# The compression network's second product behind three steps of s4, modulation out of s5, and more zero products at the seams

## The chip, the cores and the metric

The kernel runs on one core of a Trainium2 chip. The metric is device time in microseconds of one execution: the median of three runs before the change is 848.4 us (848.1, 848.4 and 856.6). Times below are us from the start of the span of one profiled execution unless said otherwise.

## The reference

Two layers work on x of 256 rows x 1024 columns in f32. One layer, cut to what matters here:

```python
h = rmsnorm(x) * (1 + scale) + shift          # scale, shift, gates: modulation, c @ adaw + adab
z = h @ w_in                                  # one input projection, its columns feed three mixers
ret  = retention(z)                           # 4 heads x 64
gmlp = spatial_gating(z)                      # 4 groups x 64, chunks of 128
nsa  = sparse_attention(z)                    # 8 query heads, 2 key heads: compressed, selected, window
x = x + gate * (concat(ret, gmlp, nsa) @ w_out)
h = rmsnorm(x) * (1 + scale2) + shift2
x = x + gate2 * experts(h)                    # 16 experts, best group of 4, top 2 in it, each 512 wide
```

The compressed branch of sparse attention runs a small network over blocks of keys and values (first product, gelu, second product) and scores the queries against its output.

## The kernel before, in words

All weights come from HBM in f32, through one queue (SP) that issues its transfers in a fixed order into a ring of eleven slots of 1 MB (`slot`, L100 to L104); a transfer waits until the readers of the slot that it overwrites are done. Further transfers of the same queue fill the experts' `wd` tiles (L1267, L1270).

A product with a weight is made of three (`mm3`, L349 to L352), since the weight and the activation are each split into a rounded part and a rest. `whl` (L338 to L347) makes the split: ACT casts the upper part (L344), DVE, or POOL for every third piece, takes the rest (L346); five such pieces can be live. The input projection is cut into pieces s0 to s5. s0 to s4 have the weight as the stationary operand and eight steps of twelve products each (`dz`); s5 has the activation stationary and 280 columns.

The order around the change, in each layer: the sum of squares (`rms_r`, L311 to L323: ACT's squares L316, PE's sums `pm` L317, ACT's logarithm L321 and exponential L322, then `hhi` L421), s0 to s3, the compression network (`comp`: first product `ph` L539, second `ph2` L544, gelu on DVE with `hid` as its result L137, third `pk` L551 with its rotary norm L357 and L360 and the values' product `pv` L564), s5, then attention. `scores(j)` (L640 to L656) makes the window scores of head pair j, `cmp_soft` (`pcs` L603) the compressed ones, `retention` its own (`pin` L695, `por` L705), `cmp_turn` transposes the compressed weights (`pct` L625), `values(j)` transposes the weights (L664, L670) and applies them (L680, L684). A string per layer, `S4P`, gives the number of s4's steps behind each half of these four rounds. Then come the output projection (`pw`), the router, the ranking of the tokens (`prank` L936 to L940), the gather (`pgx` L980), the experts (`pgu` L1051, `py` L1084) and the combination (L1123, L1131, L1310).

The modulation (c @ adaw) is cut into tasks; most are two DVE products of 128x1024 each (L193) and an addition (L194), some are PE products (L209). `FILL`, a table of digits per layer and stage, says where a task is handed out. A scheduler then orders each engine's instructions by their dependences and priorities, so the tables set priorities and not the places themselves. `WARM` times four is the number of zero products (L948) ahead of the ranking. At the seam between the layers a list `fence` names the last instructions of layer 0 on POOL, ACT and DVE; ACT's and DVE's splits of layer 1 are issued behind them.

Of the kernel before, what the change touches and what calls it, by code (L numbers as in the profile page):

```python
# [17 lines left out]
S = 256  # L18
# [22 lines left out]
OFL = True  # L41
WARM = (1, 6)
WV = (0, 1, 5)
NPA = ("0011", "0011")
S4P = ("01111111", "01111111")
WP = (3, 3)
# [16 lines left out]
         "s0 s1 s2 cmp s3 a11.0 a11.1 s5 a11.2 a11.3 s4 a12.0 a12.1 o1 o0 a12.2 a12.3".split()]  # L63
FILL = [["00000000", "00000000", "10101010", "10100000", "00", "21212121", "2222000000000000", 0],
        ["01010101", "01010101", "00000000", "00101010", "00", "10101010", "2222000000000000", 0, "000000000000000000000000"]]

# [9 lines left out]
def trunk(tc, I, out):  # L76
    nc = tc.nc
    P = 128
# [4 lines left out]
    with ctx:  # L83
# [224 lines left out]
        def tables(after):  # L308
            with tc.issue_after(after):
                exp_ln_tables()  # L310

        def rms_r(l, src, last=None):
            pm = bank("W", "pm")
            for c in range(8):
                sq = tl("k1", [S], "sq")
                sq_ = A.activation(sq, src[:, c, :], AF.Square)  # L316
                T.matmul(pm[:, :S], onesd, sq, start=c == 0, stop=c == 7)  # L317
            if last is not None:
                last(sq_.ins)
            r = tl("k1", [S], "r")  # L320
            A.activation(r, pm[:, :S], AF.Ln, bias=epsc[:, 0:1])  # L321
            A.activation(r, r, AF.Exp, scale=-0.5)  # L322
            return r  # L323
# [14 lines left out]
        def whl(wv, n):  # L338
            hl = tl("wh", [2, 512], "whl", F32R)
            hi, lo = hl[:, 0, :n], hl[:, 1, :n]  # L340
            with contextlib.ExitStack() as st:
                for i_ in fence[1:]:
                    st.enter_context(tc.issue_after(i_))
                A.copy(hi, wv)  # L344
                wc[0] += 1
                (G if wc[0] % WP[fl[0]] == 0 else V).tensor_tensor(lo, wv, hi.bitcast(F32), op=OP.subtract)  # L346
            return hi, lo  # L347

        def mm3(o, a, b, start, stop):  # L349
            T.matmul(o, a[0], b[0], start=start, stop=False, skip_group_check=True)  # L350
            T.matmul(o, a[0], b[1], start=False, stop=False, skip_group_check=True)  # L351
            T.matmul(o, a[1], b[0], start=False, stop=stop, skip_group_check=True)  # L352

# [20 lines left out]
        for l in range(L):  # L374
# [30 lines left out]
            if True:  # L405
# [33 lines left out]
                def small_loads(after):  # L439
                    with tc.issue_after(after):  # L440
                        A.dma_start(wsT, I["ws"][l].rearrange("p (g t) -> p g t", g=4))
                        A.dma_start(bsv, I["bs"][l].rearrange("p (t n) -> p t n", t=2))
                        if l == 0:
# [5 lines left out]
                                    fill=0.0, base=0, pattern=[[0, 4], [1, P]], channel_multiplier=-1)  # L449

                def dz(idx, dst_fn, tag="D"):
                    pz = [bank(tag, "pz") for _ in range(2)]

                    def step(c):
                        w = whl(ld[f"s{idx}"][c // 4][:, 512 * (c % 4):512 * (c % 4) + 512], 512)
                        for t in range(4):
                            d = slice(P * t, P * t + P)
                            mm3(pz[t // 2][:, S * (t % 2):S * (t % 2) + S], (w[0][:, d], w[1][:, d]),
                                (hhi[:, c, :], hlo[:, c, :]), c == 0 and t % 2 == 0, c == 7)
                        if c == 7:  # L460
                            for t in range(2):
                                dst_fn(2 * t, pz[t].rearrange("p (u n) -> p u n", u=2))
                    return step
# [69 lines left out]
                def comp():  # L533
# [7 lines left out]
                    raw = tl("k1", [P], "raw")  # L541
                    A.copy(raw, ph[:, :P])
                    ph2 = bank("W", "ph2")
                    T.matmul(ph2[:, :64], raw, csel.rearrange("p v g n -> p (v g n)"), start=True, stop=True)  # L544
                    hid = sml([64], "hid")
                    gelu(hid, ph2[:, :64], [64])
                    hidv = hid.rearrange("p (v g n) -> p v g n", v=2, g=2)
                    w2 = smv(l, "w2").rearrange("p (v d) -> p v d", v=2)
# [10 lines left out]
                    for g in range(2):  # L559
# [7 lines left out]
                                    hm.rearrange("p j h -> p (j h)").unsqueeze(2).to_broadcast([P, 8, 64]), op=OP.mult)  # L567
                    return bd

# [18 lines left out]

                bd = comp()
                gv = tl("t2", [2, 256], "gv")  # L590
                gat = sml([2, 24], "gat")

                def s5(tt, pz):
                    sigm(gat[:, tt, :], pz[:, 256:280])
                    gelu(gv[:, tt, :], pz[:, :256], [256])
                run(tm(5, 280, s5), lambda c: fill(FILL[l][1][c]))
                gatv = gat.rearrange("p t (h b) -> p t h b", b=3)
# [131 lines left out]
                def s4_step(n=1):  # L729
                    for _ in range(int(n)):  # L730
# [4 lines left out]
                        s4c[0] += 1  # L735

                pj = {0: scores(0)}
                cs = cmp_soft()
                for j in range(4):
# [101 lines left out]
def moe(tc, nc, l, env):  # L841
# [19 lines left out]
    if True:  # L861
# [264 lines left out]
        def combine_few(yy, pT):  # L1126
            for u in range(2):
                for i in range(2):
                    for q in range(4):
                        r_ = slice(SW * q, SW * q + SW)  # L1130
                        T.matmul(mo[q][:, S * u:S * u + S], yy[i][r_, P * u:P * u + P], pT[r_, :], start=False, stop=False,  # L1131
                                 skip_group_check=True)

# [174 lines left out]
        for m in (0, 2, 4, 6, 1, 3, 5, 7):  # L1308
            b, u = m // 2, m % 2
            last[1] = V.scalar_tensor_tensor(xT[:, m, :], mo[b][:, S * u:S * u + S], mod(l, 5)[:, m:m + 1], xT[:, m, :],  # L1310
                                   op0=OP.mult, op1=OP.add).ins
        return [last[2]] + last[:2]

# [75 lines left out]
```

## Time and profile before

| | us |
|---|---|
| median of three runs | 848.4 |
| the profiled execution | 856.05 |
| its span, first to last instruction | 854.5 |
| PE busy | 762.8 (89%) |
| DVE busy | 459.3 (54%) |
| ACT busy | 273.4 (32%) |
| POOL busy | 68.0 (8%) |
| mean granted clock of PE | 0.929 |

The profiled execution's own time stands 1.55 us above its span. PE's clock has two levels, 2.4 GHz (1.00) and 1.2 GHz (0.50); a value between is a mean over a stretch with both. "Busy" PE is PE with a product under way, at either clock. An idle time in brackets names the instruction whose end came last; a product of f32 operands appears as two records (x4 for two products).

### The profile page before, as it was taken

To read this page: it belongs to the slowest core of one execution; us is meant where nothing else is said; L and a number is where in the kernel's file an instruction comes from. 1 tells how busy PE (TensorE), PEld (TensorE's weight loads), DVE (VectorE), ACT (ScalarE), POOL (GpSimd) and SP (SyncE) were. 2 spreads that over 40 slices of the span, in tenths; PEclk is the share of its full clock that TensorE was granted. 3 is DMA by queue.
4 is the path that set the end of the run, shared out by engine and by line. 5 is a ranking of instruction groups with operands and counts; after the bars stand their busy time and mean duration, and the time that the engine had idled before them with its cause. 6 is when DMAs were issued, how large, how long until landed. Compare 5 with 4: busy or idle time off the path is not lost. (4 is left out here: it accounts for less than half of the span.)

```text
span 854.5 us, 14344 instructions
## 1 busy us (share of the span) xinstructions
PE 762.8 (89%) x5460; PEld 480.2 (56%) x5460; DVE 459.3 (54%) x1189; ACT 273.4 (32%) x655; POOL 68.0 (8%) x83
## 2 busy tenths in 40 slices
PE   3789999976999999887988998999999999979795
PEld 2677665775535455343448886678744545534342
DVE  6997959986833223211245998598582322312123
ACT  6246555633111111110135646466311201101010
POOL 2232200120000000000003231002000000000000
PEclk9899869979899999989999996699999999998798
DMA  8959818979799999999999489178878999999993
GB/s 354 420 224 354 321 45 296 395 275 383 304 381 418 417 418 419 418 420 413 421 417 379 156 300 389 58 265 323 318 283 303 359 421 415 419 418 418 416 418 145
DMA packets 47169, 292.95 MB, mean 343 GB/s; under 512 B 5488, under 2 KB 6256, under 8 KB 16496
## 3 DMA queue, kind: packets, MB, share of 16 engines
q1 hardware_dynamic: 45648, 289.76, 85.3%
q10 hardware_dynamic: 1440, 2.16, 0.8%
q8 instruction: 46, 0.75, 0.3%
q14 instruction: 35, 0.29, 0.1%
HBM read 290.84 MB, written 1.05 MB: 342 GB/s over the span
## 5 line engine op out<-in xcount | busy, mean ns | idle before, releaser
L1051 PE MATMUL pgu<-w1slot,xg 128*64 128x512 f32 x640 | 168.5, 623 | 18.3 <-PEq L1188 9.8
L1051 PEld LDWEIGHTS pgu<-w1slot,xg 128*64 128x64 f32 x640 | 51.7, 141 | 101.0 <-issue 97.9
L193 DVE SCALAR_TENSOR_TENSOR adaslot<-adaslot,sb__90 128x1024 f32<-128x1024 f32 x72 | 94.5, 1324 | 0.0
L1093 DVE SCALAR_TENSOR_TENSOR yy<-py,gc,yy 64x512 fp32r<-64x512 f32 x40 | 30.0, 750 | 108.6 <-ACT yy L1092 108.6
L350 PE MATMUL pz<-hhi,whl 128*128 128x256 f32 x256 | 75.0, 304 | 10.2 <-ACT hhi L421 10.2
L351 PE MATMUL pz<-hlo,whl 128*128 128x256 f32 x256 | 76.1, 301 | 0.9 <-DVE hlo L422 0.7
L352 PE MATMUL pz<-hhi,whl 128*128 128x256 f32 x256 | 76.3, 304 | 0.5 <-DVE whl L346 0.4
L1092 ACT ACTIVATE yy<-py,gc 64x512 fp32r<-64x512 f32 x40 | 27.3, 683 | 151.5 <-PE py L1084 135.3
L346 POOL TENSOR_TENSOR whl<-winslot,whl 128x512 fp32r<-128x512 f32 (+1 forms) x24 | 34.2, 1425 | 370.7 <-DMA winslot<-win_dram 239.7
L1060 PE MATMUL pgu<-w1slot,xg 128*32 128x256 f32 x896 | 58.4, 382 | 5.2 <-DMA w1slot<-w_dram 5.2
L350 PEld LDWEIGHTS pz<-hhi,whl 128*128 128x128 f32 x256 | 51.1, 205 | 14.4 <-ACT hhi L421 13.1
L351 PEld LDWEIGHTS pz<-hlo,whl 128*128 128x128 f32 x256 | 52.5, 205 | 3.0 <-DVE hlo L422 1.7
L352 PEld LDWEIGHTS pz<-hhi,whl 128*128 128x128 f32 x256 | 51.9, 204 | 3.6 <-issue 2.1
L1040 DVE CAST pgT<-ppg 128x256 fp32r<-128x256 f32 x34 | 14.4, 424 | 72.3 <-PE ppg L1038 72.3
L344 ACT CAST whl<-winslot 128x512 fp32r<-128x512 f32 (+1 forms) x72 | 40.7, 576 | 26.6 <-PE pz L352 25.4
L1067 DVE TENSOR_TENSOR a<-a,pgu 128x256 f32<-128x256 f32 (+1 forms) x34 | 12.4, 365 | 65.6 <-ACT a L1066 65.4
L1060 PEld LDWEIGHTS pgu<-w1slot,xg 128*32 128x32 f32 x896 | 28.6, 109 | 33.8 <-issue 16.5
L1066 ACT ACTIVATE a<-pgu 128x256 f32<-128x256 f32 (+1 forms) x34 | 11.6, 340 | 108.4 <-PE pgu L1051 91.7
L350 PE MATMUL pw<-yhi,whl 128*128 128x256 f32 x128 | 37.6, 295 | 5.5 <-DVE mod L194 3.9
L1101 ACT ACTIVATE yy<-py,gc 128x256 fp32r<-128x256 f32 x14 | 6.6, 473 | 108.6 <-PE py L1109 108.6
L346 DVE TENSOR_TENSOR whl<-winslot,whl 128x512 fp32r<-128x512 f32 (+1 forms) x48 | 33.7, 707 | 10.0 <-ACT whl L344 9.9
L352 PE MATMUL pw<-yhi,whl 128*128 128x256 f32 x128 | 36.9, 295 | 2.3 <-DVE whl L346 2.2
(506 smaller groups left out, 1455.7 us busy)
## 6 DMA issues: line engine op xcount, KB each, us to landing
w1slot<-w_dram SPq DMA_DIRECT2D x128, 1024.0 KB, 16.2
adaslot<-adaw_dram SPq DMA_DIRECT2D x40, 1024.0 KB, 7.0
wd<-wd_dram SPq DMA_DIRECT2D x30, 1024.0 KB, 14.7
winslot<-win_dram SPq DMA_DIRECT2D x14, 1024.0 KB, 16.1
slot<-adaw_dram SPq DMA_DIRECT2D x8, 1024.0 KB, 18.5
woslot<-wout_dram SPq DMA_DIRECT2D x8, 1024.0 KB, 11.6
slot<-win_dram SPq DMA_DIRECT2D x6, 1024.0 KB, 17.5
cmpslot<-cmpw_dram SPq DMA_DIRECT2D x4, 1024.0 KB, 13.5
```

The lines of the kernel that those rows point to most:

```text
L193: V.scalar_tensor_tensor(wb, wb, 1.0, sb_, op0=OP.mult, op1=OP.mult, accum_out=mv_[:, b:b + 1])
L344: A.copy(hi, wv)
L346: (G if wc[0] % WP[fl[0]] == 0 else V).tensor_tensor(lo, wv, hi.bitcast(F32), op=OP.subtract)
L350: T.matmul(o, a[0], b[0], start=start, stop=False, skip_group_check=True)
L351: T.matmul(o, a[0], b[1], start=False, stop=False, skip_group_check=True)
L352: T.matmul(o, a[1], b[0], start=False, stop=stop, skip_group_check=True)
L1040: V.tensor_copy(pT, pp_[:, :S])
L1051: lastu[0] = T.matmul(gu[64 * j:64 * j + 64, :], xg(c)[:, xs:xs + CAP], w1(c, j), start=c == 0, stop=c == 7, skip_group_check=True).ins
L1060: lastu[0] = T.matmul(gu[SW * t:SW * t + SW, 0:256], xg(c)[:, xs:xs + SW], wv, start=c == 0, stop=c == 7, skip_group_check=True).ins
L1067: V.tensor_tensor(a, a, gu[:, n:2 * n], op=OP.mult)
L1092: ya = A.activation(y[0:64, :], py[r_, :], AF.Copy, scale=gc[r_, :])
L1093: V.scalar_tensor_tensor(y[64:128, :], py[r_, :], gc[r_, :], y[0:64, :].bitcast(F32), op0=OP.mult, op1=OP.subtract)
```

## The change

The second half of the compression network moves. `comp` becomes a generator of three parts: the first product before s5; the second product and the gelu after the first step of s5; `pk` and what follows behind three steps of s4 that now stand before scores(0), with a fence on the last product of the third. A fourth step of s4 follows scores(0), and three more are left for the rounds. `FILL` takes the modulation out of s5 in layer 1 and hands tasks out between s4's steps. `WARM` makes 24 zero products of 4 in layer 0, and 32 of 24 in layer 1. A new helper `spin` puts three zero products ahead of the seam's sums of squares and eight behind them. The fence of the splits on ACT is now the last of the eight squares.

```diff
-WARM = (1, 6)
+WARM = (6, 8)
-S4P = ("01111111", "01111111")
+S4P = ("11010000", "11010000")
-FILL = [["00000000", "00000000", "10101010", "10100000", "00", "21212121", "2222000000000000", 0],
-        ["01010101", "01010101", "00000000", "00101010", "00", "10101010", "2222000000000000", 0, "000000000000000000000000"]]
+FILL = [["00000000", "00000000", "00001111", "10100000", "00", "21212121", "2222000000000000", 0],
+        ["01010101", "00000000", "00010111", "00101010", "00", "10101010", "2222000000000000", 0, "000000000000000000000000"]]
...
+        def spin(n, after):
+            wz = bank("W", "wz")
+            with tc.issue_after(after):
+                for _ in range(n):
+                    T.matmul(wz, zb, zb.unsqueeze(1).to_broadcast([P, 4, P]), start=True, stop=True, skip_group_check=True)
+
         def rms_r(l, src, last=None):
+            if fence:
+                spin(3, fence[3])
             pm = bank("W", "pm")
             for c in range(8):
                 sq = tl("k1", [S], "sq")
                 sq_ = A.activation(sq, src[:, c, :], AF.Square)
-                T.matmul(pm[:, :S], onesd, sq, start=c == 0, stop=c == 7)
+                pm_ = T.matmul(pm[:, :S], onesd, sq, start=c == 0, stop=c == 7)
             if last is not None:
                 last(sq_.ins)
+            if fence:
+                fence[1] = sq_.ins
+                spin(8, pm_.ins)
...
-                for i_ in fence[1:]:
+                for i_ in fence[1:3]:
...
                     raw = tl("k1", [P], "raw")
                     A.copy(raw, ph[:, :P])
+                    yield
                     ph2 = bank("W", "ph2")
                     T.matmul(ph2[:, :64], raw, csel.rearrange("p v g n -> p (v g n)"), start=True, stop=True)
                     hid = sml([64], "hid")
                     gelu(hid, ph2[:, :64], [64])
+                    yield
                     hidv = hid.rearrange("p (v g n) -> p v g n", v=2, g=2)
...
-                bd = comp()
+                bds = []
+                cgen = comp()
+                next(cgen)
...
-                run(tm(5, 280, s5), lambda c: fill(FILL[l][1][c]))
+
+                def comp_step(c):
+                    if c == 0:
+                        next(cgen)
+                run(tm(5, 280, s5), lambda c: fill(FILL[l][1][c]), comp_step)
...
+                s4_step(3)
+                with tc.issue_after(ls4[0]):
+                    next(cgen, None)
+                bd = bds[0]
                 pj = {0: scores(0)}
+                s4_step(1)
                 cs = cmp_soft()
...
-        return [last[2]] + last[:2]
+        return [last[2]] + last[:2] + [lastu[0]]
```

`lastu[0]` is the last product of the combination; `ls4[0]` is the last product that `mm3` returned in a step. Line numbers below 300 are the same in both kernels; further down those of the changed one are 8 to 26 higher.

PE's order in layer 0 between s5 (`pz<-whl,hlo`) and the first scores (`sc<-kr,qn`); before:

```order
L352 MATMUL pz<-whl,hlo 128x280
L695 MATMUL pin_1242<-rr 128x256
L551 MATMUL pk<-hid,sm_67 64x15 x2
L695 MATMUL pin_1243<-rr 128x256
L357 MATMUL pr<-zc,pg 128x15
L360 MATMUL pm_1020<-sqc,bo 128x15
L695 MATMUL pin_1242<-rr 128x128
L695 MATMUL pin_1243<-rr 128x128
L564 MATMUL pv<-sm_67,hvr 128x64
L640 MATMUL sc_1142<-kr,qn 128x256
```

and after, where `pz<-hhi,whl` and `pz<-hlo,whl` are s4's products (twelve such groups of three stand ahead of `pk`, three behind it):

```order
L363 MATMUL pz<-whl,hlo 128x280
L361 MATMUL pz<-hhi,whl 128x256
L362 MATMUL pz<-hlo,whl 128x256
L363 MATMUL pz<-hhi,whl 128x256
...
L566 MATMUL pk<-hid,sm_67 64x15 x2
...
L368 MATMUL pr<-zc,pg 128x15
L371 MATMUL pm_1167<-sqc,bo 128x15
L579 MATMUL pv<-sm_67,hvr 128x64
L661 MATMUL sc_1189<-kr,qn 128x256
```

36 products of s4 have moved ahead of `pk`, and retention's products (`pin`) behind the scores. Up to the first `pct` there are 72 products of s4 (31 before) in layer 0 and 81 (28 before) in layer 1.

SP's order in layer 0 ahead of the experts' first weights (`w1slot`), where `adaslot` is the modulation's, `woslot` the output projection's; before:

```order
L103 DMA winslot<-win_dram 128x2048 x2
L103 DMA adaslot<-adaw_dram 128x2048 x9
L1267 DMA wd__2185<-wd_dram 128x1024
L103 DMA adaslot<-adaw_dram 128x2048
L103 DMA woslot<-wout_dram 128x2048 x4
L103 DMA adaslot<-adaw_dram 128x2048 x12
L103 DMA w1slot<-w_dram 128x2048 x4
L1267 DMA wd__2187<-wd_dram 128x1024
```

and after, where the same tile is `wd__2205` by its new number:

```order
L103 DMA winslot<-win_dram 128x2048 x2
L103 DMA adaslot<-adaw_dram 128x2048 x10
L103 DMA woslot<-wout_dram 128x2048 x4
L103 DMA adaslot<-adaw_dram 128x2048 x12
L103 DMA w1slot<-w_dram 128x2048 x4
L1293 DMA wd__2205<-wd_dram 128x1024
L1293 DMA wd__2207<-wd_dram 128x1024
```

The issue of that tile has moved behind 17 slots of the modulation and the output projection and four of the experts.

ACT's order at the seam between the layers, where `sq<-xT` are the squares, `whl<-winslot` the splits' casts, `r` the logarithm and the exponential; before:

```order
L344 CAST whl<-winslot 128x512 x2
L316 ACTIVATE sq<-xT 128x256
L344 CAST whl<-winslot 128x512 x2
L316 ACTIVATE sq<-xT 128x256 x7
L140 ACT_TABLE_LOAD
L344 CAST whl<-winslot 128x512
L321 ACTIVATE r<-pm,epsc 128x256
L322 ACTIVATE r<-r 128x256
L421 ACTIVATE hhi<-ht,mod_118 128x256 x6
```

and after:

```order
L324 ACTIVATE sq<-xT 128x256 x8
L140 ACT_TABLE_LOAD
L355 CAST whl<-winslot 128x512
L332 ACTIVATE r<-pm,epsc 128x256
L355 CAST whl<-winslot 128x512
L333 ACTIVATE r<-r 128x256
L355 CAST whl<-winslot 128x512 x2
L432 ACTIVATE hhi<-ht,mod_118 128x256 x4
```

The eight squares stand together; the four casts that stood among them are behind.

## Rows read from the trace of the kernel before

**Rows 1.** Busy time by stage: us, engines busy (instructions), PE's clock, DMA share, GB/s.
```profile
98.00:128.00 30.00, 28.64 (x109) 17.45 (x109) 20.00 (x62) 16.10 (x63) 1.60 (x2) 0.66 0.37 155
128.00:168.00 40.00, 39.17 (x307) 27.87 (x305) 37.53 (x96) 24.89 (x76) 2.89 (x3) 1.00 0.90 341
...
222.00:441.00 219.00, 201.28 (x1553) 98.28 (x1549) 64.76 (x204) 30.08 (x58) 0.00 (x0) 0.98 1.00 407
...
518.00:552.00 34.00, 31.18 (x115) 21.23 (x115) 21.79 (x67) 19.49 (x70) 4.46 (x3) 0.60 0.46 182
```
**Rows 2.** PE's timeline, layer 0: start, length, operation, [idle before <-releaser].
```profile
97.94 0.29 PE L352 MATMUL pz<-whl,hlo 128*128 128x280 f32 x1
...
100.21 0.29 PE L551 MATMUL pk<-hid,sm 128*64 128x15 f32 x4 [1.35 <-DVE hid L137]
...
103.37 1.23 PE L640 MATMUL sc<-kr,qn 64*128 64x256 f32 x4
...
109.59 3.46 PE L603 MATMUL pcs<-kcr,qn 128*128 128x32 f32 x16
...
123.57 0.28 PE L350 MATMUL pz<-hhi,whl 128*128 128x256 f32 x1
123.68 0.28 PE L351 MATMUL pz<-hlo,whl 128*128 128x256 f32 x1
...
128.14 0.38 PE L625 MATMUL pct<-ident,cs 128*128 128x128 f32 x2
...
133.87 0.70 PE L640 MATMUL sc<-kr,qn 64*128 64x256 f32 x4
...
136.24 1.05 PE L209 MATMUL pad<-adaslot,scol 128*32 128x512 f32 x2
```
**Rows 3.** PE's timeline, layer 1, s5's last product, pk and pct.
```profile
517.41 0.29 PE L352 MATMUL pz<-whl,hlo 128*128 128x280 f32 x1
...
520.83 0.38 PE L551 MATMUL pk<-hid,sm 128*64 128x15 f32 x4 [3.12 <-DVE hid L137]
...
552.45 0.38 PE L625 MATMUL pct<-ident,cs 128*128 128x128 f32 x2
```
**Rows 4.** DVE's timeline, a split of s4 (layer 0) and the modulation ahead of hid (layer 1).
```profile
99.34 0.68 DVE L346 TENSOR_TENSOR whl<-winslot,whl 128x512 fp32r<-128x512 f32 x1
...
519.32 1.21 DVE L193 SCALAR_TENSOR_TENSOR adaslot<-adaslot,sb__90 128x1024 f32<-128x1024 f32 x1
```
**Rows 5.** Waits of SP's queue: us in total, times, longest.
```profile
SPq L103 <- DVE adaslot L193: 100.8, 24, 27.6
...
SPq L1267 <- PE pin L695: 23.1, 1, 23.1
```
**Rows 6.** PE's timeline at the entry to the experts, both layers.
```profile
209.88 0.38 PE L948 MATMUL mo<-zb 128*128 128x512 bf16 x1 [0.73 <-DVE lg L873]
213.90 0.17 PE L936 MATMUL prank<-o,ub 128*128 128x16 bf16 x1 [3.64 <-DVE o L924]
...
221.52 1.07 PE L1051 MATMUL pgu<-w1slot,xg 128*64 128x512 f32 x3
...
613.58 4.69 PE L948 MATMUL mo<-zb 128*128 128x512 bf16 x21
618.71 0.17 PE L936 MATMUL prank<-o,ub 128*128 128x16 bf16 x1 [0.44 <-DVE o L924]
...
623.98 0.65 PE L1051 MATMUL pgu<-w1slot,xg 128*64 128x512 f32 x2
```
**Rows 7.** Timelines of ACT and PE at the seam between the layers.
```profile
450.18 0.47 ACT L321 ACTIVATE r<-pm,epsc 128x256 f32<-128x256 f32 x1 [1.30 <-PE pm L317]
...
452.21 0.50 PE L350 MATMUL pz<-hhi,whl 128*128 128x256 f32 x2 [2.07 <-ACT hhi L421]
...
455.80 0.39 PE L350 MATMUL pz<-hhi,whl 128*128 128x256 f32 x1
```
**Rows 8.** Busy time in a stretch of layer 1 with PE idle for 1.45 us.
```profile
616.00:620.00 4.00, 2.55 (x17) 1.14 (x15) 3.76 (x32) 2.03 (x4) 0.00 (x0) 1.00 0.97 359
```

More of the change, by code (lines that the diff above doesn't have):

```diff
@@ L351, in mm3 @@
             T.matmul(o, a[0], b[1], start=False, stop=False, skip_group_check=True)
-            T.matmul(o, a[1], b[0], start=False, stop=stop, skip_group_check=True)
+            return T.matmul(o, a[1], b[0], start=False, stop=stop, skip_group_check=True).ins
         def rope_norm(pool, xs, sq, n, nt, gcol, pg, cos, sin, outs, sumidx, eps):
@@ L449, in small_loads @@
                                     fill=0.0, base=0, pattern=[[0, 4], [1, P]], channel_multiplier=-1)
+                ls4 = [None]
                 def dz(idx, dst_fn, tag="D"):
@@ L457, in step @@
                             d = slice(P * t, P * t + P)
-                            mm3(pz[t // 2][:, S * (t % 2):S * (t % 2) + S], (w[0][:, d], w[1][:, d]),
-                                (hhi[:, c, :], hlo[:, c, :]), c == 0 and t % 2 == 0, c == 7)
+                            ls4[0] = mm3(pz[t // 2][:, S * (t % 2):S * (t % 2) + S], (w[0][:, d], w[1][:, d]),
+                                         (hhi[:, c, :], hlo[:, c, :]), c == 0 and t % 2 == 0, c == 7)
                         if c == 7:
@@ L567, in comp @@
                                     hm.rearrange("p j h -> p (j h)").unsqueeze(2).to_broadcast([P, 8, 64]), op=OP.mult)
-                    return bd
+                    bds.append(bd)
                 if l or LK < 1:
@@ L1130, in combine_few @@
                         r_ = slice(SW * q, SW * q + SW)
-                        T.matmul(mo[q][:, S * u:S * u + S], yy[i][r_, P * u:P * u + P], pT[r_, :], start=False, stop=False,
-                                 skip_group_check=True)
+                        lastu[0] = T.matmul(mo[q][:, S * u:S * u + S], yy[i][r_, P * u:P * u + P], pT[r_, :], start=False,
+                                            stop=False, skip_group_check=True).ins
         def extras():
```

## The prediction

> **What bounds the kernel now.** I read the busy times by stage first, then PE's timeline where a stage's clock is low, then the waits of PE and SP there. In [rows 1] the expert stage of layer 0 (222 to 441 us) moves 407 GB/s with the DMA engines busy 1.00 of the time: the weight stream bounds it, and the diff changes neither it nor its like in layer 1. What can move is what lies before each stream: the stream's first product comes as soon as attention and routing let it, and the stream then runs its own length. Two stretches there stand out. From 98 to 128 us PE is "busy" 28.64 of 30 us at a granted clock of 0.66, while DVE has 20.00 us of work and the DMA engines 0.37. From 518 to 552 us it is the same in layer 1: PE 31.18 of 34 us at clock 0.60, DVE 21.79, DMA 0.46. So there PE is full only because it runs at 1.2 GHz, and no other engine is near its limit. Right behind, from 128 to 168 us, PE has 39.17 of 40 us at clock 1.00 and DVE 37.53: both nearly full, so a gain made before is carried through, and not much more is to be had.
>
> PE's timeline [rows 2] shows how the first stretch begins: the last product of s5 starts at 97.94 (0.29 us), and pk of the compression network starts at 100.21 after 1.35 us of waiting for DVE's hid (the products of retention between them are short). What follows is narrow (15 columns) and then the scores, and all of this runs at half clock: scores(0) takes 103.37 to 109.59 = 6.2 us; the same four products of scores(2) at full clock take 133.87 to 136.24 = 2.4 us. In layer 1 [rows 3] s5's products stop at 517.41 and pk waits 3.12 us for hid; the transposes of the weights (pct) that end the stretch come at 552.45. On DVE [rows 4] hid stands behind a modulation product of 1.21 us (at 519.32).
>
> **The change part by part.** The sums are against the profiled execution, 856.05 us (span 854.5 and 1.55 us around it); it lies 7.6 us (0.9%) above the median of the three runs, 848.4, and the saving is carried to the median in us.
>
> *Layer 0, opening of attention.* pk no longer stands behind s5, but behind three steps of s4, 36 products. At full clock these start 0.115 us apart (123.57 and 123.68, [rows 2]), so they fill 36 x 0.115 = 4.1 us, from 98.2 to 102.3, past the time at which hid is there today (pk starts at 100.21). Up to the first pct 72 products of s4 now stand in PE's order, 31 before: 41 x 0.115 = 4.7 us of work is brought forward. If the clock stays at 2.4 GHz, the stretch from s5's end (98.2) to pct (128.14, 29.9 us) changes as follows: scores(0) and (1) 2 x (6.2 - 2.4) = -7.6; pcs, which the timeline has at 3.46 us at half clock, halves, -1.7; the pause, -1.35; of the 31 old products of s4 some 14 run at half clock, where the spacing is about double, 14 x 0.1 = -1.4; pr, pm, pv and the first products of retention about -0.8; the products brought forward, +4.7. Sum -8.2. DVE sets a floor: it has 20.0 us in the 30 [rows 1], and 41 products are 3.4 splits more, of which two in three are DVE's, 2.3 x 0.68 = 1.6 us (one of 0.68 stands in [rows 4]). 21.6 us of work in a chain that also waits for PE makes at most 8 us of gain. I take -8, between 0 (the clock falls anyway) and -10 (the work brought forward also shortens 128 to 168 us).
>
> *The same in layer 1.* s5's end (517.70) to pct (552.45) is 34.7 us. The pause of 3.12 us shrinks to about 1.2, since s5's own last split on DVE ends only where the modulation product begins, at 519.32 [rows 4]: about -1.9. Twelve s5 products, the first pin, pcs, both scores and small ones at full clock: about -1.3, -1.4, -1.7, -4.9, -1.0; 25 of the 28 old s4 products x 0.1: -2.5; 53 products brought forward (81 for 28): +6.1. Sum -8.6; because the pause left over can still cost some of the clock I take -7, between 0 and -12. The modulation is taken out of s5 by the table, but the order shows nearly the same modulation products up to pct as before (DVE is the engine that limits s5, and those products had been squeezed out of it anyway): the cost of this edit is put at 0, with 2 x 1.21 us for one task pushed into attention as its bound.
>
> *DMA.* SP's queue stood 23.1 us in one wait for a product of retention, before the issue of a wd tile [rows 5]; behind it waited a modulation slot, four slots of the output projection and twelve more. This issue now stands behind them, so the stream of weights is free some 20 us earlier. It is worth 0 by itself, since PE and DVE end later than those loads; but it is the cover under the 8 us: without it the output projection's weights, queued behind the wait, would be late for an earlier attention. The remaining 100.8 us of waits for DVE's modulation products [rows 5] lie under PE's and DVE's work.
>
> *Entry to the experts.* Layer 0 gets 24 zero products for 4, all before the ranking. PE waits 3.64 us for DVE before prank (213.90) and its gathers then run at half clock: from prank to the first expert product at 221.52 are 7.6 us; layer 1, with 24 zero products, takes 618.71 to 623.98 = 5.3 us [rows 6]. So -2.3. The 20 added take 20 x 0.22 (4.69 us for 21, [rows 6]) = 4.5 us, in waits of 0.73 + 3.64 = 4.4: hidden to within 0.1 us, at most +1 if DVE is early. Layer 1 gets 32, of which 28 stand before prank: 4 x 0.22 = 0.9 against a wait of 0.44: +0.4, bounds 0 and 0.9.
>
> *The seam.* Three zero products before the sums of squares and eight behind them lie in PE's waits for ACT. ACT's splits go behind the eight squares, so the logarithm (450.18, after a wait of 1.30 for PE) comes some 2 us earlier: four of the five splits that stood before it are gone, and three now stand between it and the first hhi. The first product of s0 waited 2.07 us for hhi, and s0 ran at half clock for 3.6 us (452.21 to 455.80, [rows 7]), -1.8 at most. Bounds +1 (the splits are now late for s0) and -3.5; I take -1.5, near the ACT chain alone.
>
> Sum: -8 - 7 - 2.3 + 0.4 - 1.5 = -18.4 us. From 848.4: **830.0 us**.
>
> **Rivals.**
> - *The clock falls in layer 1 all the same* (the pause of 1.2 us stays). For: in layer 0 a pause of 1.35 us was enough. Against: in 616 to 620 us PE was idle 1.45 of 4 us and the clock stayed at 1.00 [rows 8]. Only the pause (1.9 us) is then won in layer 1: 830.0 + 7 - 1.9 = 835 us.
> - *The gain is given back behind pct.* The products of s4 that were the filling between scores(2), (3) and the values are used up. If PE falls to 1.2 GHz for 10 us of its work in each layer, that costs up to 2 x 5 us: 840 us. For: 41 and 53 products are gone from there. Against: DVE is nearly full there and hides part; modulation on PE remains as filling.
> - *It ends slower.* The same mechanism, in its place 128 to 168 us and 552 to 600 us, all along it: PE has 39.17 us in the first, so half clock over 12 us of work more per layer brings +24 - 18.4 = +5.6: 854 us. It decides from 9.2 us per layer lost behind pct. Against it: there the clock was 1.00 throughout [rows 1], and 24 and 15 of the 96 products of s4 still lie there. The Trainium skill, "TensorE: Matmul & The Clock Gate", Part 4 "PE-mode transpose", speaks for it: transposes do not count as busy for the clock in the way of other products, and the values are full of transposes. By that rule alone the 854 us would be the forecast; the trace has the transposes between products of s4 with the clock at full, so it does not bear the rule out for this mixture and cannot show it for one without them.
> - *It doesn't do what it says:* with s4's splits ahead of it on DVE and ACT hid is late again and PE waits at pk after the three steps, at half clock. Then only the entries and the seam count: 848.4 - 3.4 = 845 us.
>
> **How the numbers follow.** Forecast 0.62, layer 1's clock 0.14 (835), given back 0.12 (840), nothing gained in attention 0.07 (845), slower 0.05 (854). A measurement of this kernel tells about 1% from no change, 8.5 us, so faster is below 839.9: all but a little of the first two and half of the third, 0.81; same 0.13; slower 0.06, with something for what I did not see. The likeliest case's own range, by the bounds of its terms: -8 to -10, -5 to -12, -2 to -2.6, +0.9 to 0, 0 to -3.5, that is 834 to 820. To leave out no more than 2 in 10 the upper end goes to the third case and part of the fourth, 844; the lower end to 818.
>
> **What would show it.** Right: clock near 1.00 over the stretch from s5's end to pct in both layers, pk with no wait for hid, that stretch about 22 us (layer 0) and 27 us (layer 1) long; gathers of layer 0 in 4 us; no 23 us wait of SP; the two expert stages as long as before. Wrong: a granted clock of 0.5 at the scores, or at the values behind pct; a longer wait of PE for splits in s4's first steps; a longer stretch from pct to the output projection, which would mean that DVE, not PE, sets it.

## The result and the profile after

The changed kernel takes 861.7 us (median of four runs, 855.9 to 862.3) against 848.25 for the kernel before: a ratio of 1.0143, 95% interval 1.0096 to 1.019. It is slower by 1.4%, where 830 us and a gain of 2.2% were forecast. Ratios here and below are estimated from executions within 1.5% of their kernel's fastest and are not the quotients of the medians. The profiled execution has a span of 860.7 us, so it speaks for the median, as that of the kernel before (854.5 us) does not.

By stage (busy time of PE, PE's weight loads, DVE, ACT, POOL, then PE's clock, DMA share, GB/s), the rows of the changed kernel that answer to [rows 1], with the two on either side of the seam:

```profile
98.00:128.00 30.00, 28.32 (x132) 18.77 (x132) 22.94 (x68) 17.03 (x64) 2.56 (x2) 0.72 0.53 220
128.00:168.00 40.00, 38.91 (x263) 24.34 (x262) 32.89 (x82) 22.82 (x69) 3.62 (x2) 1.00 0.76 273
...
222.00:441.00 219.00, 203.21 (x1551) 97.37 (x1547) 64.43 (x203) 29.70 (x56) 0.00 (x0) 0.97 1.00 407
441.00:456.00 15.00, 10.74 (x71) 7.38 (x68) 10.11 (x22) 10.11 (x22) 2.82 (x2) 1.00 1.01 421
456.00:518.00 62.00, 56.31 (x400) 47.39 (x402) 53.59 (x91) 31.30 (x59) 17.49 (x12) 0.97 0.72 256
518.00:552.00 34.00, 31.19 (x191) 22.15 (x184) 28.53 (x70) 18.11 (x63) 4.52 (x3) 0.80 0.77 304
```

The expert stage is what it was. The clock of the first opening rose only from 0.66 to 0.72, that of the second from 0.60 to 0.80. And a stretch that the forecast had not looked at is worse: from 456 to 518 us PE is busy 56.31 of 62 us. In the kernel before it was:

```profile
456.00:518.00 62.00, 60.95 (x460) 51.97 (x458) 55.02 (x93) 31.75 (x62) 18.30 (x12) 1.00 0.75 274
```

PE's timeline of layer 0 answers to [rows 2] (start, length, operation, [idle before <-releaser]):

```profile
102.61 0.29 PE L566 MATMUL pk<-hid,sm 128*64 128x15 f32 x4
...
105.03 0.40 PE L368 MATMUL pr<-zc,pg 128*128 128x15 f32 x2 [0.87 <-ACT zc L569]
...
107.48 2.07 PE L661 MATMUL sc<-kr,qn 64*128 64x512 f32 x2 [0.45 <-DVE rnb L380]
...
112.66 3.46 PE L624 MATMUL pcs<-kcr,qn 128*128 128x32 f32 x16
...
131.59 0.38 PE L646 MATMUL pct<-ident,cs 128*128 128x128 f32 x2
```

The pause ahead of pk is gone, as forecast, and s4's products run at full clock up to 104 us. But two pauses of 0.87 and 0.45 us follow, the scores behind them take 2.07 us as they did at half clock, and pcs takes the same 3.46 us as in [rows 2]. The granted clock is 1.00 up to 104 us and then falls:

```profile
104.00:108.00 4.00, 2.68 (x15) 1.82 (x14) 4.00 (x11) 2.14 (x9) 1.27 (x1) 0.92 1.01 424
108.00:112.00 4.00, 4.00 (x10) 1.25 (x8) 2.73 (x10) 3.17 (x14) 0.00 (x0) 0.50 1.01 416
```

It is back at full only at some 124 us. So pct comes at 131.59 and not at 128.14. In layer 1 pct comes at 557.83 (552.45 in [rows 3]).

At the entries to the experts (rows that answer to [rows 6]):

```profile
215.88 0.17 PE L962 MATMUL prank<-o,ub 128*128 128x16 bf16 x1 [0.44 <-DVE o L950]
...
221.16 1.94 PE L1077 MATMUL pgu<-w1slot,xg 128*64 128x512 f32 x8
```

From prank to the first expert product are 5.3 us, 7.6 before: the forecast's -2.3. Layer 0 had lost 2.0 us by then, so the experts of layer 0 begin at nearly the same time, 221.2 for 221.5 us. The rest of the loss arises behind them. At the seam, PE and DVE:

```profile
452.36 0.50 PE L361 MATMUL pz<-hhi,whl 128*128 128x256 f32 x2 [1.81 <-ACT hhi L432]
453.40 0.38 PE L362 MATMUL pz<-hlo,whl 128*128 128x256 f32 x1 [0.54 <-DVE hlo L433]
459.40 0.58 PE L363 MATMUL pz<-hhi,whl 128*128 128x256 f32 x1 [2.78 <-DVE whl L357]
```

```profile
449.29 0.69 DVE L357 TENSOR_TENSOR whl<-winslot,whl 128x512 fp32r<-128x512 f32 x1 [3.08 <-ACT whl L355]
...
458.67 2.48 DVE L357 TENSOR_TENSOR whl<-winslot,whl 128x512 fp32r<-128x512 f32 x4
```

s0 starts when it did (452.36 for 452.21 in [rows 7]), and then stops for 2.78 us on the rest of a split; behind the stop the granted clock is 0.71 (460 to 464 us). In the kernel before DVE makes three of these rests in a time in which it has nothing else:

```profile
445.75 1.89 DVE L346 TENSOR_TENSOR whl<-winslot,whl 128x512 fp32r<-128x512 f32 x3
451.13 1.28 DVE L420 SCALAR_TENSOR_TENSOR ht<-xT,gs,r 128x256 f32<-128x256 f32 x3 [3.49 <-ACT r L322]
```

With ACT's casts behind the squares, DVE waits 3.08 us for a cast instead, makes one rest, then the normalised input, and the other rests come at 458.67, behind it. From the start of DVE's last combination instruction (`yy`) of layer 0 to the compression network's first product in layer 1 are 69.8 us before and 75.0 after. This is called the seam's stretch below.

### The profile page after: what moved, and what is told of

Its sections match the earlier page's. It is cut to its first block, busy times and chain, and to the rows that moved or that the text cites. A ratio compares the mean times of both kernels' runs of the same rounds, so it can differ in the third digit from the quotient of the medians.

```text
span 860.7 us, 14438 instructions
## 1 busy us (share of the span) xinstructions
PE 768.2 (89%) x5499; PEld 474.6 (55%) x5499; DVE 464.6 (54%) x1189; ACT 274.7 (32%) x655; POOL 69.3 (8%) x83
## 5 line engine op out<-in xcount | busy, mean ns | idle before, releaser
L193 DVE SCALAR_TENSOR_TENSOR adaslot<-adaslot,sb__90 128x1024 f32<-128x1024 f32 x72 | 91.4, 1283 | 0.0
L361 PE MATMUL pz<-hhi,whl 128*128 128x256 f32 x256 | 74.0, 300 | 9.8 <-ACT hhi L432 9.8
L363 PE MATMUL pz<-hhi,whl 128*128 128x256 f32 x256 | 75.2, 299 | 4.5 <-DVE whl L357 4.3
L1086 PE MATMUL pgu<-w1slot,xg 128*32 128x256 f32 x896 | 58.4, 382 | 2.7 <-DMA w1slot<-w_dram 2.7
L357 DVE TENSOR_TENSOR whl<-winslot,whl 128x512 fp32r<-128x512 f32 (+1 forms) x48 | 37.8, 797 | 15.2 <-ACT whl L355 15.2
```

The source lines that it names most:

```text
L193: V.scalar_tensor_tensor(wb, wb, 1.0, sb_, op0=OP.mult, op1=OP.mult, accum_out=mv_[:, b:b + 1])
L363: return T.matmul(o, a[1], b[0], start=False, stop=stop, skip_group_check=True).ins
L1086: lastu[0] = T.matmul(gu[SW * t:SW * t + SW, 0:256], xg(c)[:, xs:xs + SW], wv, start=c == 0, stop=c == 7, skip_group_check=True).ins
```

## The experiments

Two theories stood: the fence on ACT's splits costs the time at the seam; or the reordered attention costs it and the seam only shows it. The third question was what the clock does in the two openings. All ratios are to the kernel before on the same chip.

**The fence undone.** In the changed kernel:

```diff
             if fence:
-                fence[1] = sq_.ins
                 spin(8, pm_.ins)
```

> The changed kernel with ACT's splits of layer 1 again behind the last instruction of the combination, not behind the eight squares. Theory (the fence moves three rests of splits out of DVE's idle time at the seam, and PE then waits 2.8 us for one): that wait is gone, the compression network's first product of layer 1 comes 4 to 6 us earlier against s0's chain in the changed kernel, and the time is 4 to 6 us below the changed kernel's, 856 to 858 us, beside a kernel before at 848. Rival (the loss sits in the reordered attention; the seam only moves it): within 2 us of the changed kernel, 860 to 862.

Measured: 850.2 us, ratio 1.0022 (0.9976 to 1.0069). Below the 856 to 858 us that the theory asked for: against the changed kernel's ratio of 1.0143 the fence makes up 1.2%. The seam shows it on DVE:

```profile
443.74 1.88 DVE L356 TENSOR_TENSOR whl<-winslot,whl 128x512 fp32r<-128x512 f32 x3
447.72 1.62 DVE L430 SCALAR_TENSOR_TENSOR ht<-xT,gs,r 128x256 f32<-128x256 f32 x3 [2.10 <-ACT r L332]
```

The three rests are back in DVE's empty time, PE's wait of 2.78 us in s0 is gone, and the seam's stretch is 67.2 us, 7.8 less than in the changed kernel and 2.6 less than before. In this kernel's profile the clock also came back earlier in both openings (table below). In layer 0 that cannot be the fence's doing: the fence does not reach there, PE and DVE have the same order in both kernels, and still pk to pct takes 24.5 us for 29.0. It is a difference between executions.

**The attention alone.** The kernel before with the moved compression network, s4's steps and the table; `WARM`, `spin` and the fence as before.

> The kernel before with only the moved compression network, the moved steps of s4 and the modulation's table; no zero products added, no fence. Theory (fence): about the kernel before, 0 to +3 us, since the clock falls in both openings all the same. Rival (the reordered attention is what costs): +5 to +9 us against the kernel before. My forecast of step one would want -15.

Measured: 857.1 us, ratio 1.0092 (1.0049 to 1.0135). So the rival holds as well: the reordering costs some 8 us by itself. Neither theory alone is right; both parts cost, and the zero products pay a part back. With the two runs that follow, the fence alone (+4.7 us) and the zero products alone (-2.5), the parts sum to +10.0 us, where the ratio of the changed kernel is worth some 12; the intervals leave room for the 2.

**The fence alone,** in the kernel before:

```diff
             if last is not None:
                 last(sq_.ins)
+            if fence:
+                fence[1] = sq_.ins
```

> The kernel before with the new fence of ACT's splits alone. Theory (fence): +4 to +6 us against the kernel before, with a wait of 2 to 3 us of PE for a split's rest in s0. Rival (attention): 0 to +1 us.

Measured: 852.6 us, ratio 1.0055 (1.0021 to 1.0088), +4.7 us. The seam's stretch grows from 69.8 to 74.6 us, nearly as much as in the changed kernel. PE's wait for the split's rest is 1.14 us here, less than expected, but the first hhi is late as well:

```profile
453.97 0.50 PE L352 MATMUL pz<-hhi,whl 128*128 128x256 f32 x2 [3.24 <-ACT hhi L423]
...
461.01 0.38 PE L354 MATMUL pz<-hhi,whl 128*128 128x256 f32 x1 [1.14 <-DVE whl L348]
```

**The entries alone.** `WARM = (6, 8)` in the kernel before.

> The kernel before with the zero products at the two entries to the experts alone (24 and 32 for 4 and 24). By the sum of the forecast: -2.3 in layer 0, +0.4 in layer 1, so -1 to -3 us against the kernel before. Rival (the stream of weights, not the gathers, decides when the experts begin): 0.

Measured: 849.8 us (median of all its runs; 848.1 for the kernel before beside it), ratio 0.9949 (0.9895 to 1.0003): not clear of nothing in time. The profile is clear: 5.3 us from prank to the first expert product in layer 0, for 7.6. This kernel also gave a line that was not looked for. Its attention has the order of before, instruction by instruction; yet in layer 1:

```profile
527.47 0.29 PE L551 MATMUL pk<-hid,sm 128*64 128x15 f32 x4 [3.13 <-DVE hid L137]
...
549.98 0.38 PE L625 MATMUL pct<-ident,cs 128*128 128x128 f32 x2
```

After the same pause of 3.1 us the stretch from pk to pct takes 22.5 us, not 31.6 as in [rows 3]; the granted clock is 0.85 over it, and was 0.58 over the same stretch of the kernel before:

```profile
527.00:550.00 23.00, 22.48 (x117) 15.76 (x118) 19.81 (x61) 17.90 (x67) 4.15 (x3) 0.85 0.51 212
```

```profile
521.00:553.00 32.00, 32.00 (x122) 21.92 (x120) 19.79 (x62) 17.95 (x66) 3.81 (x3) 0.58 0.40 157
```

How long the clock stays down there differs between executions with one order of instructions. The zero products alone, with the same order of PE in both layers, also take 22.5 us, and the fence alone, whose order differs a little here, 22.3. In layer 0 the kernel of this experiment shows it the other way: 33.3 us for the 27.9 of before.

**The attention alone, with the old table.** As the attention alone, with `FILL` of before.

> The attention part alone (compression network and steps of s4 moved, no zero products added, no fence) with the kernel before's table for the modulation. Theory (order: with s4's products spent early, the rounds of scores and values in layer 1 are a chain of short steps between DVE and PE with nothing to fill it): the loss stays, +5 to +9 us against the kernel before, and PE waits over 2 us for DVE at a po or ptp of layer 1. Rival (table: the modulation taken out of s5 and put into attention makes DVE late there): 0 to +2 us.

Measured: 856.7 us, ratio 1.009 (1.0055 to 1.0125), the same as with the new table. The modulation's table does nothing that can be measured; it is the order of s4 and the compression network, which were not tried apart. The wait that was looked for is there, 2.7 us at `po` of layer 1.

**The steps of s4 kept for the later rounds.** As the attention alone, with

```diff
-S4P = ("11010000", "11010000")
+S4P = ("00001111", "00001111")
...
-                s4_step(1)
```

> The attention part alone, as changed, but the fourth step of s4 not behind scores(0) and the steps that remain given to the last four half rounds (00001111) in place of the first ones. Theory (order): the filling is back between the values, so most of the loss goes, 0 to +3 us against the kernel before. Rival (table, or the moved compression network itself): +5 to +9 us as with the attention part alone.

Measured: 868.0 us, ratio 1.0189 (1.0126 to 1.0252): the theory behind it fell, and in an instructive way. In the profiled execution, which at 874.5 us is the slowest of its six, the first rounds of scores have no product of s4 among them, and PE is at half clock for most of the way to pct in both layers:

```profile
98.00:128.00 30.00, 28.09 (x102) 16.55 (x103) 19.09 (x53) 14.83 (x57) 2.56 (x2) 0.63 0.53 218
...
538.00:570.00 32.00, 30.93 (x118) 20.17 (x117) 18.32 (x58) 15.55 (x55) 2.54 (x2) 0.63 0.42 165
```

The stretch from pk to pct takes 35.4 and 31.9 us. By the medians, 868.0 against 856.7 us, s4's products are worth more among the first scores than between the values; that they are so because they bring the clock back rests on this one profile.

**The zero products alone.** Entries and seam, order of attention and fence as before.

> The kernel before with all zero products of the change (24 and 32 at the experts' entries, 3 and 8 at the seam), the order of attention and the fence as before. Theory (the zero products are what is worth having in the change): -3 to -6 us against the kernel before, 842 to 845 us: -2.3 at the entry in layer 0, -2 to -4 at the seam. Rival (the seam's products are given back in the stretch where DVE is full): -1 to -2.5 us.

Measured: 845.8 us, ratio 0.997 (0.9938 to 1.0001), -2.5 us by the ratio: near the rival, at the lower end of what was looked for. The seam's stretch takes 67.3 us for 69.8, so the products at the seam bring 2.5 us in the profile, and the entries 2.3. The seam's stretch differs between executions too: it takes 68.0 to 72.0 us in the five profiles with the old fence and no zero products at the seam, 67.2 to 68.1 in the seven with the old fence and these products. With the new fence it is 74.6 us without them and 75.0 with them: there they gain nothing, so undoing the fence in the changed kernel gave more at the seam (7.8 us) than adding it to the kernel before cost (4.8).

**Zero products among the scores.** The zero products alone, and

```diff
-                            T.matmul(scv[g][:, :, n - P:n], identb, trib, start=False, stop=True, skip_group_check=True)
+                            tr_ = T.matmul(scv[g][:, :, n - P:n], identb, trib, start=False, stop=True, skip_group_check=True)
+                            if j < 2 and g == 1:
+                                spin(4, tr_.ins)
```

> The same with four more zero products behind each pair of masked scores of the first two rounds, 32 in all, 0.22 us each. Theory (in both openings PE's clock falls in the sparse scores, in layer 0 always, in layer 1 in some executions; denser work holds it): the granted clock stays near 1.00 from the scores to pct, that stretch shrinks by 4 to 6 us in layer 0 for 3.5 us of added work, and the time is 2 to 5 us below that of the zero products without these. Rival (the clock falls by the pause ahead of pk, not by the scores): clock at 0.5 all the same, and +3 us.

Measured: 838.4 us, ratio 0.9865 (0.9807 to 0.9923). Here is the clock in the opening of layer 0, four us to a row:

```profile
100.00:104.00 4.00, 4.00 (x22) 2.56 (x23) 4.00 (x9) 1.63 (x7) 1.27 (x1) 0.67 1.01 426
104.00:108.00 4.00, 4.00 (x10) 1.22 (x8) 2.57 (x10) 2.68 (x12) 0.00 (x0) 0.50 1.00 420
108.00:112.00 4.00, 3.86 (x27) 2.78 (x25) 2.21 (x7) 1.62 (x8) 0.00 (x0) 0.98 0.21 88
112.00:116.00 4.00, 4.00 (x20) 1.86 (x19) 3.87 (x16) 3.66 (x14) 0.00 (x0) 1.00 0.01 2
```

The zero products do not keep the clock from falling behind the pause; they bring it back at 108 us. With the zero products at the entries and the seam alone it came back after 120:

```profile
116.00:120.00 4.00, 4.00 (x14) 2.27 (x12) 2.12 (x9) 2.51 (x10) 0.00 (x0) 0.50 0.00 0
120.00:124.00 4.00, 4.00 (x17) 2.90 (x17) 3.71 (x15) 2.28 (x7) 0.00 (x0) 0.62 0.01 4
```

pk to pct takes 23.2 us for 28.0, though ten of s4's products have gone behind pct (21 for 31 ahead of it), and from pct to the last product of the output projection it takes 79.2 us for 76.4. The pause lets the clock go, the sparse scores keep it down: the theory was half right. The two profiled executions are only 0.8 us apart (839.3 and 840.1 us), since that of the kernel without these products is the fastest of its twelve. Where the 7.4 us between the medians come from is to be seen in the granted clocks of all executions: over the whole span they are 0.936 to 0.950 without these products and 0.960 to 0.964 in all six with them.

**The reordering with the clock helped.** The changed kernel, fence undone, with the same zero products among the scores.

> The changed kernel with the fence undone and the same four zero products behind each pair of masked scores of the first two rounds. It differs from the kernel with zero products at the entries, the seam and the scores (838.4 us) by the moved compression network, the moved steps of s4 and the table alone. Theory (the reordering itself costs, by the later pk and by a stretch behind pct that does not shrink, whatever the clock does): 5 to 9 us above that kernel, 843 to 848 us. Rival (the reordering costs only because the clock is lost; with the clock held it wins what I forecast): at or below 838 us.

Measured: 841.3 us, ratio 0.9944 (0.9917 to 0.997); between the two expectations, 3 us by the medians above the kernel with the old order, with intervals that overlap a little. The profile parts the layers (table): from ph to the last product of the output projection the reordering wins in layer 0 (108.6 us for 111.5) and loses in layer 1 (96.6 for 92.1).

**Two zero products for four** in the kernel with the old order.

> Zero products at the entries, the seam and the scores, order of attention and fence as before, but two instead of four behind each pair of scores. Theory (they work by making PE's work denser, so fewer bring the clock back later): between the kernel with none there (845.8) and that with four (838.4), 840 to 844 us, with pk to pct of layer 0 at 24 to 28 us. Rival (any product there is enough; four only add work): 836 to 838 us.

Measured: 837.8 us, ratio 0.9871 (0.9803 to 0.9939), as with four. The rival's number came, but its one profile shows layer 0 at half clock until past 120 us all the same, pk to pct 30.4 us. One profile does not say how often that is so; whether two are enough stays open.

**In all four rounds.** As the kernel with four, but `j < 4`.

> Four zero products behind each pair of masked scores of all four rounds, everything else as in the kernel with them in two rounds (838.4 us). Theory (behind pct the clock is at 1.00 without them and DVE is nearly full, so they buy nothing there and cost up to 16 x 2 x 0.11 = 3.5 us in the two layers): 838 to 842 us. Rival (PE's clock is lost there too in some executions): 835 to 837 us.

Measured: 844.3 us, ratio 0.9932 (0.9889 to 0.9974). The expectation's price was half of what it should have been: 32 more products at 0.22 us each are 7.0 us, not 3.5. In the profile pct to the last product of the output projection grows from 59.5 to 62.6 us in layer 1 and shrinks from 79.2 to 78.1 in layer 0. In the kernel with them in two rounds the clock behind pct is 1.00 in layer 1, and in layer 0 up to 168 us, so in the later rounds there is nothing to buy. But this profile is one of the three executions near 840 us, with a clock of 0.968 over the whole span; the eight at 844 to 849 us have 0.950 to 0.962. Where the clock is lost in those no profile shows.

**The reordering in layer 0 alone,** zero products at the entries, the seam and the first scores, no fence, layer 1 in the old order and with its old table:

```diff
-S4P = ("11010000", "11010000")
+S4P = ("11010000", "01111111")
...
                 next(cgen)
+                if l:
+                    for _ in cgen:
+                        pass
...
-                s4_step(3)
-                with tc.issue_after(ls4[0]):
-                    next(cgen, None)
+                if not l:
+                    s4_step(3)
+                    with tc.issue_after(ls4[0]):
+                        next(cgen, None)
```

> Zero products at the entries, the seam and the scores, no fence; the moved compression network, steps of s4 and table in layer 0 alone, layer 1 in the order of before. Theory (with the clock held the reordering wins in layer 0, where the last product of the output projection came at 199.1 against 202.4 us, and loses in layer 1, where DVE is full until pk and the three steps' splits are late: +4.5 us): 3 us below the kernel with the order of before and the same zero products, 834 to 837 us, under both kernels. Rival (the reordering loses or wins nothing in either layer): 838 to 842 us.

Measured: 835.0 us, ratio 0.9825 (0.977 to 0.9881), as expected, and 1.75% under the kernel before. That is clear of the kernel with both layers reordered (0.9917 to 0.997), and not clear of the one with the old order in both (0.9807 to 0.9923). Its openings:

```profile
98.00:128.00 30.00, 28.67 (x174) 18.39 (x174) 26.79 (x77) 18.93 (x67) 2.58 (x3) 0.94 0.61 246
518.00:552.00 34.00, 33.63 (x223) 23.22 (x222) 32.02 (x90) 25.05 (x91) 3.68 (x2) 1.00 0.57 189
```

The clock is at 0.94 and 1.00 (0.66 and 0.60 in [rows 1]), and DVE now has 26.79 of 30 and 32.02 of 34 us beside PE's 28.67 and 33.63: both are nearly full, and little is left to be had there.

The stretches of all of them, in us from start to start of PE's products (ph: first product of the compression network; pw: last product of the output projection), each from one profile:

| kernel | L0 ph-pk | pk-pct | pct-pw | L1 ph-pk | pk-pct | pct-pw |
|---|---|---|---|---|---|---|
| before | 9.1 | 27.9 | 77.2 | 9.6 | 31.6 | 57.6 |
| entries alone | 9.2 | 33.3 | 78.0 | 9.6 | 22.5 | 58.4 |
| fence alone | 9.1 | 27.9 | 77.1 | 11.2 | 22.3 | 57.2 |
| zero products alone | 9.2 | 28.0 | 76.4 | 9.6 | 22.5 | 58.3 |
| two zeros for four | 9.2 | 30.4 | 76.8 | 9.6 | 22.4 | 58.1 |
| zeros and scores | 9.1 | 23.2 | 79.2 | 9.6 | 23.0 | 59.5 |
| in all four rounds | 9.2 | 23.1 | 78.1 | 9.6 | 23.0 | 62.6 |
| changed | 12.1 | 29.0 | 75.7 | 13.9 | 27.1 | 59.1 |
| fence undone | 12.1 | 24.5 | 77.8 | 16.0 | 21.0 | 60.7 |
| attention alone | 12.1 | 29.1 | 75.7 | 16.0 | 22.9 | 59.7 |
| the same, old table | 12.1 | 27.9 | 77.5 | 16.0 | 27.1 | 60.3 |
| steps kept | 12.1 | 35.4 | 73.6 | 16.0 | 31.9 | 59.4 |
| reordered, zeros and scores | 12.1 | 23.5 | 73.0 | 16.0 | 22.4 | 58.2 |
| reordered in layer 0 alone | 12.1 | 23.2 | 71.6 | 9.6 | 21.6 | 59.1 |

With four zero products at the first scores pk to pct of layer 0 takes 23.1 to 23.5 us in all four profiles; without them, or with two, it takes 24.5 to 35.4 in ten. The sums of a row's three parts show where the reordering costs without those four. In layer 0 it makes no clear difference: 114.4 to 117.5 us in the changed kernel, the fence undone and the attention alone with either table, 113.6 to 120.5 in the old order. In layer 1 it does: 97.7 to 103.4 us, against 90.1 to 90.7 in four of the five profiles with the old order; the fifth, 98.8, is that of the kernel before.

## Why the prediction was wrong, point by point

Three of its terms failed: layer 0's opening (-8 forecast), layer 1's (-7) and the seam (-1.5). Between the two profiles layer 0 lost 2.6 us from ph to the last product of the output projection, layer 1 lost 1.3, the seam's stretch 5.2, and the entry of layer 0 gave back 2.3; that is the difference of the spans, 854.5 to 860.7 us, to within a microsecond. Against the 90.4 us that layer 1 takes with the zero products alone, in the order of before, it lost 9.7 instead, and the sum, some 15 us, is near the 13.5 by which the medians differ.

**"The clock stays at 2.4 GHz" (layer 0, -8 us).** This step failed. pk did lose its wait, and s4's products did run at full clock. But behind pk the same narrow products and scores follow, with pauses of 0.87 and 0.45 us, and the clock fell there: pk to pct is 29.0 us in the changed kernel for 27.9 (24.5 to 29.1 in three profiles with this order, 27.9 to 33.3 in four with the old one). The forecast had put the fall down to the pause and gave the case that the clock falls anyway only as the end of a range, without a price for the scores by themselves. The 3.0 us by which pk is later are then simply lost. With zero products among the scores some of the forecast's gain appears, ph to the last product of the output projection being 108.6 us reordered (12.1 + 23.5 + 73.0) and 111.5 in the old order: 3 us, not 8.

**"The same in layer 1" (-7 us).** Two things were wrong. First, the stretch of 31.6 us was a trait of the one profiled execution. With the same order of PE's instructions it takes 22.5 us in two other kernels, and next to nothing was to be won there. The profiled execution was 7.6 us above the median, and the forecast said so and then carried its saving to the median in full; that difference should have been looked for in the stretches at half clock first. Second, the three steps of s4 ahead of pk are not free here, since DVE is full up to that point and makes the splits; the forecast read DVE's 21.79 of 34 us, a mean over the whole stretch, as room. In the changed kernel:

```profile
520.00:524.00 4.00, 3.21 (x26) 2.98 (x24) 4.00 (x6) 1.48 (x3) 1.62 (x1) 1.00 0.96 360
524.00:528.00 4.00, 2.97 (x24) 2.97 (x25) 4.00 (x11) 2.86 (x11) 0.53 (x1) 1.00 1.01 426
528.00:532.00 4.00, 4.00 (x36) 3.67 (x34) 4.00 (x8) 3.00 (x9) 1.10 (x1) 1.00 1.01 426
```

DVE has 4.00 of 4 us while PE waits in the first two rows. Of these waits the longest, 1.83 us, is for the rest of a split. pk comes 16.0 us behind ph in the reordered kernels with no fence, 9.6 in the old order; 36 products at 0.115 us would have been 4.1. The last experiment bears this out: with layer 1 put back the kernel is clearly faster than with both layers reordered.

**"A gain made before is carried through."** The 41 and 53 products brought forward should have shortened the stretch behind pct or at least been neutral. In layer 0 it shrank by 1.5 us (77.2 to 75.7) in the changed kernel, in layer 1 it grew by 1.5. There the values' rounds are a chain through DVE, and without s4's products PE idles in it:

```profile
572.00:576.00 4.00, 1.66 (x14) 1.33 (x16) 4.00 (x10) 1.90 (x4) 0.66 (x1) 0.87 0.78 268
576.00:580.00 4.00, 4.00 (x18) 1.61 (x14) 2.61 (x8) 0.89 (x4) 0.00 (x0) 0.70 0.98 346
```

```profile
574.34 2.25 PE L701 MATMUL po<-pT,vt 128*64 128x256 f32 x16 [2.98 <-DVE mod L194]
```

The rival that had the kernel slower by that mechanism had the right place and a part of the price, but the clock's part of it in layer 1 was small: the clock fell in these two rows, behind PE's idle time, and not for whole rounds. The Trainium skill, "TensorE: Matmul & The Clock Gate", Part 4 "PE-mode transpose", has transposes not count as busy in the way of other products. For this mixture that was not borne out: behind pct of layer 1 the reordered kernel with zero products among the scores kept 1.00 in every row from 540 to 580 us, with the transposes of the values and 24 products of s4 among them. What transposes by themselves do no run here shows.

**"The seam" (-1.5 us, at most +1).** The logarithm did come earlier (449.16 for 450.18), and from 441 to 456 us the clock was 1.00 for 0.77 before. But the bound of +1, which the sum of the range then took as 0, was far off: the seam's stretch grew by 5.2 us (69.8 to 75.0). The fence alone costs 4.7 us; the zero products alone gain about 2.5 at that place, and beside the fence nothing. The forecast followed ACT's chain only, and did not ask what else a cast on ACT feeds. It feeds a rest on DVE, which had 5.3 us with nothing else to do just there (445.8 to 451.1 us) and hardly any afterwards.

**"Entry to the experts" (-2.3 and +0.4).** Right in layer 0, 7.6 to 5.3 us. In layer 1 the stretch from the output projection's last product to the first expert product went from 13.9 to 14.0 us, +0.1 for +0.4.

**DMA, and the table.** SP's wait of 23.1 us for a product of retention is gone as forecast, but the stream did not come free by it. SP now waits 21.8 us for a modulation product of PE (`pad`) between the first and the second slot of the output projection; waits for `pad` were 4.3 us in total before. The first slot of layer 0's experts is issued at 183.5 us, 180.8 before.

```profile
SPq L103 <- PE pad L209: 27.9, 4, 21.8
```

The table cost nothing, as forecast (1.0092 and 1.009 with and without it).

## What to carry to other kernels

Before a loss at half clock is put into a sum, look whether the profiled execution is a usual one: a clock that falls after a short pause stays down for different times in different executions, and a median a few us below the profile is a sign of it. Products brought forward to fill a pause want their inputs earlier too; ask which engine makes these inputs and whether it has time there, and do so for each stage apart, since the same move, with the clock helped, won 3 us in layer 0 and lost 4.5 in layer 1 by the profiles. An instruction fenced off one engine's path also moves what waits for it on another, out of idle time that may not come again.

## What the runs showed of the hardware

One order of PE's instructions took 31.6 us in one execution and 22.5 in two others from pk to pct of layer 1, after the same pause of 3.1 us, with granted clocks of 0.58 and 0.85 in two of them; in layer 0 one order took 27.9 to 33.3. The Trainium skill, "TensorE: Matmul & The Clock Gate", Part 1, section "What's actually happening", has the number of slow products at a kernel's start vary from run to run for one kernel; these rows, in the middle of one, show the same kind of difference. And products of zeros, 0.22 us each at full clock and read by nobody, sixteen of them in an opening, brought the clock of layer 0 back at 108 us for some 123. The clock over the whole span was 0.960 to 0.964 in the six executions with them and 0.936 to 0.950 in the twelve without, and the medians 838.4 and 845.8 us.
